# Experts of a routed feed-forward layer rebuilt: one set of 64 places for a pair, weights in 4 KB pieces

## Chip, cores and metric

The kernel runs on one core of one Trainium2 chip. The number that counts is the device time of one execution, in microseconds (us). Work is spread over the core's engines: PE (matrix products; PEld is its loading of the stationary operand), DVE and ACT (elementwise work), POOL, and SP, whose queue issues nearly all transfers from memory (HBM). Sixteen DMA engines move the data. Products land in PSUM banks (128 partitions x 512 float32) and are read from there by DVE or ACT.

## What is computed

One layer over 256 tokens of width 1024. Its first half (norm, input products, stick-breaking attention, retention, gated output products) is not touched by the change. The second half is a mixture of 16 experts in 4 groups: a token picks its best group and in it its best two experts, and the result is normed once more.

```python
    group_probs = jax.nn.softmax(group_logits, axis=-1)
    p_group, g_sel = lax.top_k(group_probs, 1)
...
    top_vals, top_idx = lax.top_k(in_group, TOP_K_IN_GROUP)
    gate = jax.nn.softmax(top_vals, axis=-1) * p_group
    expert_id = g_sel * EXPERTS_PER_GROUP + top_idx
    combine = jnp.sum(jax.nn.one_hot(expert_id, N_EXPERTS, dtype=jnp.float32) * gate[..., None], axis=1)
...
    for e in range(N_EXPERTS):
        hidden = jax.nn.silu(xt @ w_exp_gate[e]) * (xt @ w_exp_up[e])
        y = y + combine[:, e:e + 1] * (hidden @ w_exp_down[e])
...
    return rms_norm(h, norm_final_g)
```

Each expert has two weights of 1024 x 512 (gate, up) and one of 512 x 1024 (down), in float32: 6.3 MB an expert, 100.7 MB for all 16. Every expert's weights are read once, whatever the routing.

## The kernel before

**Memory and loads.** On-chip memory is cut into 25 slots of 8 KB a partition (1 MB), handed out first freed, first used (`take`, `give`). All weights are split into tiles of one slot. `plan` puts a tile on a list in the order of its use, and `pump` issues the next ones on SP's queue (L161) as long as slots are free; a tile's slot is freed (`drop`) by the last product that reads it. While the dense half runs, the table `LIMIT` caps how many tiles are loaded; after the routing the cap is lifted (L861). The experts' tiles follow the dense ones: for each pair of experts 4 tiles of gate, 4 of up, 4 of down, 96 in all. A tile holds 256 rows of both experts of the pair, as two DMAs of 512 KB (`both`, L444). Partition p takes rows p and 128+p of the 256, so each contiguous piece in memory is one row of 512 numbers, 2 KB. The last tile is cut into four DMAs. Eight DMAs are in flight at most.

**Routing.** From the logits DVE makes a 0/1 mask of the chosen experts, PE counts them by a product with a triangular table, and `rank` gives each token its place in each expert (64 places, `CAP`). `onehot` turns ranks into 0/1 matrices `pt` for four experts at a time. `cnt` is the largest count of an expert (L875).

**The experts**, two at a time (`experts`, `up_to_hidden`), in the order of the code, which is the order on every engine:

- `gather` (L893) multiplies the rows by `pt` and puts the rows of four experts x 64 places, transposed, into `xgt`. The first two pairs' rows come from the float32 rows themselves (`gather_pair`, L906), the later ones from rows in two parts `hn` (`rows_in_parts`).
- `proj` (L961) makes the gate product and then the up product. The two experts of the pair stand in the two halves of one bank (64 partitions each): 16 matmuls a product, 32 records in the trace, since each float32 matmul makes two.
- `place_shares` (L942) gives each place its row's norm and its share; ACT applies silu (L1017), DVE multiplies with the up product (L1049), PE transposes the hidden rows (L1054) and ACT copies them out (L1055). `place_table` (L935) transposes the 0/1 matrix for the way back (L939, L940).
- `down` (L980) makes the two halves of 512 columns one after the other, each into its own bank, again with the two experts in the two halves of the partitions. `split_y` splits each bank in two parts `y2` (ACT L546, DVE L547).
- `scatter` (L997) multiplies by the table and adds a pair's rows onto four banks `F` that hold the running sum; a pair's scatter stands between the next pair's up and down products.

After seven pairs the engines read `cnt` into a register and `tc.If(most > CAP)` (L1147) decides over further rounds for an expert of more than 64 tokens. The eighth pair and the final norm stand behind that block, so that every engine passes it:

```python
    experts(True)
...
    most = nc.values_load(cnt[0:1, 0:1], min_val=0, max_val=T)
    assert not loads
    with tc.If(most > CAP):
...
    ht = up_to_hidden(NP - 1, final_gain)
```

At the end each of the four quarters of the sum (two blocks of tokens `tb`, two halves of columns `q`) is squared by ACT (L1177), the norm is a power on POOL (L1196), and ACT and DVE scale the rows that two queues store (L1201 to L1204).

Of the kernel before, what the change touches and what calls it, by code (L numbers as in the profile page):

```python
# [9 lines left out]
F32 = mybir.dt.float32  # L10
# [17 lines left out]
# weight tiles loaded by the start of a unit of the dense products, at most  # L28
# [6 lines left out]
# columns of the packed constant table (one row per partition)  # L35
# [35 lines left out]
# columns of the packed parameters  # L71
# [7 lines left out]
R_N = 228  # L79


def pack(ins):
# [9 lines left out]
        ins["norm_final_g"].reshape(8, P).T,  # L92
    ], axis=1))
# [3 lines left out]
def layer(ctx: ExitStack, tc, cst, dec, prm, x, w_in, w_gate, w_sb_out, w_ret_out,  # L97
# [108 lines left out]
    units = []  # L206

    def dense_a(tag, w, c0, ncol, rhs, evac, nk=KC):
        """out^T [cols, tokens]: weights stationary, tokens moving."""
# [10 lines left out]
    def dense_b(tag, w, c0, widths, lhs, evac, pieces=1, hook=None):  # L220
        """out [tokens, cols]: tokens stationary, weights moving."""
# [222 lines left out]
    def both(w, i, r, cs, cut=False):  # L444
        """256 rows of the weights of a pair of experts."""
        e = [rows(w[0, 2 * i + j], 256 * r, 2, cs.start, 512) for j in range(2)]
        if cut:
            return [((slice(None), j, k), e[j][:, k]) for k in range(2) for j in range(2)]
        return [((slice(None), j), e[j]) for j in range(2)]

    for i in range(NE // 2):
        for which, w in (("g", w_exp_gate), ("u", w_exp_up)):
            for r in range(4):
                plan((which, i, r), [P, 2, 2, 512], both(w, i, r, slice(0, 512)))
        for q in range(2):
            for r in range(2):
                plan(("d", i, q, r), [P, 2, 2, 512], both(w_exp_down, i, r, slice(512 * q, 512 * q + 512),
                                                          (i, q, r) == (NE // 2 - 1, 1, 1)))
    n_expert = 12 * (NE // 2)
    expert_loads = loads[-n_expert:]  # L460

# [499 lines left out]
    def proj(i, which, ps, ahead=None):  # L961
        for r in range(4):
            if ahead:
                ahead(r)
# [263 lines left out]
```

## Time and profile before

| | |
|---|---|
| median of 3 runs | 484.58 us (484.14 to 484.59) |
| span of the profiled execution | 482.5 us |
| around the span (484.58 - 482.5) | 2.1 us |
| busy share of the span: PE, PEld, DVE, ACT, POOL | 96%, 65%, 41%, 35%, 5% |
| mean granted PE clock, as a share of full speed | 0.987 |
| read from HBM | 140.93 MB |
| experts (first gather to the end) | 249.4 to 482.5 us |

The page gives each engine's busy share, then the span in 40 slices with the granted PE clock and the DMA traffic. PE is busy in nearly every slice. That alone doesn't say that PE sets the time: records of matmuls are pipelined, and a stage is read from its waits. In the slices from 300 to 446 us the DMA engines move 386 to 388 GB/s without a break; then they stop before the end, while the chain of work that ended last runs over PE.

### The profile page before, as it was taken

To read this page: it belongs to the slowest core of one execution; us is meant where nothing else is said; L and a number is where in the kernel's file an instruction comes from. 1 tells how busy PE (TensorE), PEld (TensorE's weight loads), DVE (VectorE), ACT (ScalarE), POOL (GpSimd) and SP (SyncE) were. 2 spreads that over 40 slices of the span, in tenths; PEclk is the share of its full clock that TensorE was granted. 3 is DMA by queue.
4 is the path that set the end of the run, shared out by engine and by line. 5 is a ranking of instruction groups with operands and counts; after the bars stand their busy time and mean duration, and the time that the engine had idled before them with its cause. 6 is when DMAs were issued, how large, how long until landed. Compare 5 with 4: busy or idle time off the path is not lost. (4 is left out here: it accounts for less than half of the span.)

```text
span 482.5 us, 6985 instructions
## 1 busy us (share of the span) xinstructions
PE 462.2 (96%) x2799; PEld 314.4 (65%) x2799; DVE 199.4 (41%) x370; ACT 170.5 (35%) x247; POOL 21.9 (5%) x36
## 2 busy tenths in 40 slices
PE   7899999999999999999999999999999999994993
PEld 6699778888899999999974444543353436341231
DVE  3756488454467755786363121412121112111003
ACT  3633787876555654445321113011010101110023
POOL 2300111000012000000010000000000000000000
PEclk9999999999999999999999999999999999998897
DMA  7999975248020599977998999999999999999902
GB/s 276 353 384 395 383 248 175 88 122 314 1 88 1 185 351 387 385 263 254 392 316 298 382 332 378 386 385 387 387 387 387 386 388 386 387 387 385 337 0 88
DMA packets 83143, 142.51 MB, mean 295 GB/s; under 512 B 3872, under 2 KB 24480, under 8 KB 82976
## 3 DMA queue, kind: packets, MB, share of 16 engines
q1 hardware_dynamic: 82672, 141.35, 82.3%
q10 hardware_dynamic: 432, 0.64, 0.4%
q8 instruction: 24, 0.39, 0.3%
q14 instruction: 15, 0.12, 0.1%
HBM read 140.93 MB, written 1.05 MB: 294 GB/s over the span
## 5 line engine op out<-in xcount | busy, mean ns | idle before, releaser
L970 PE MATMUL p<-b,b 128*64 128x512 f32 x512 | 116.4, 603 | 7.3 <-PEq L1147 6.2
L251 DVE TENSOR_TENSOR b<-b,b 128x1024 fp32r<-128x1024 f32 x72 | 88.7, 1240 | 71.8 <-ACT b L249 70.7
L292 PE MATMUL p<-b,b 128*128 128x512 f32 (+1 forms) x504 | 102.4, 358 | 0.7 <-ACT b L249 0.5
L249 ACT ACTIVATE b<-b 128x1024 fp32r<-128x1024 f32 x72 | 75.5, 1056 | 77.3 <-PE p L280 46.0
L292 PEld LDWEIGHTS p<-b,b 128*128 128x128 f32 x504 | 82.3, 189 | 14.8 <-ACT b L249 0.9
L970 PEld LDWEIGHTS p<-b,b 128*64 128x64 f32 x512 | 36.0, 138 | 76.0 <-issue 72.6
L279 PE MATMUL p<-b,b 128*128 128x256 f32 x288 | 71.6, 286 | 0.0
L280 PE MATMUL p<-b,b 128*128 128x256 f32 x288 | 70.7, 283 | 0.0
L985 PE MATMUL p<-b,b 128*64 128x512 f32 x256 | 56.7, 595 | 0.0
L279 PEld LDWEIGHTS p<-b,b 128*128 128x128 f32 x288 | 55.1, 191 | 0.5
L280 PEld LDWEIGHTS p<-b,b 128*128 128x128 f32 x288 | 55.2, 192 | 0.0
L282 PE MATMUL p<-b,b 128*128 128x256 f32 x288 | 41.1, 283 | 0.0
L985 PEld LDWEIGHTS p<-b,b 128*64 128x64 f32 x256 | 17.7, 137 | 32.9 <-issue 30.5
L282 PEld LDWEIGHTS p<-b,b 128*128 128x128 f32 x288 | 37.4, 192 | 0.0
L547 DVE SCALAR_TENSOR_TENSOR b<-p,b 128x512 fp32r<-128x512 f32 (+1 forms) x20 | 12.7, 635 | 57.5 <-ACT b L546 53.6
L1017 ACT ACTIVATE b<-p,share 128x512 f32<-128x512 f32 x8 | 5.5, 688 | 75.2 <-DVE share L949 75.2
L546 ACT ACTIVATE b<-p 128x512 fp32r<-128x512 f32 (+1 forms) x20 | 11.0, 552 | 54.9 <-PE p L985 54.2
L1049 DVE SCALAR_TENSOR_TENSOR b<-p,share,b 128x512 f32<-128x512 f32 x8 | 6.0, 751 | 49.1 <-PE p L970 49.1
L1055 ACT ACTIVATE b<-p 128x512 f32<-128x512 f32 x8 | 4.8, 599 | 52.2 <-PE p L1054 52.2
L949 DVE TENSOR_REDUCE share<-p 128x3 f32<-128x9 f32 x8 | 1.3, 167 | 43.6 <-PE p L946 43.6
L1001 PE MATMUL p<-b,S 128*128 128x512 f32 x64 | 19.1, 420 | 0.3
L1001 PEld LDWEIGHTS p<-b,S 128*128 128x128 f32 x64 | 10.8, 188 | 9.1 <-issue 6.5
(171 smaller groups left out, 357.9 us busy)
## 6 DMA issues: line engine op xcount, KB each, us to landing
b<-in_w_exp_gate SPq DMA_DIRECT2D x64, 512.0 KB, 10.8
b<-in_w_exp_up SPq DMA_DIRECT2D x64, 512.0 KB, 10.8
b<-in_w_exp_down SPq DMA_DIRECT2D x62, 512.0 KB, 10.7
b<-in_w_in SPq DMA_DIRECT2D x17, 1024.0 KB, 14.5
b<-in_w_gate SPq DMA_DIRECT2D x8, 1024.0 KB, 5.3
b<-in_w_ret_out SPq DMA_DIRECT2D x4, 1024.0 KB, 4.9
b<-in_w_out SPq DMA_DIRECT2D x4, 1024.0 KB, 11.0
b<-in_w_sb_out SPq DMA_DIRECT2D x2, 1024.0 KB, 9.3
```

What stands on the lines that cost most here:

```text
L249: act.activation(hi, raw, AF.Copy)
L251: tt(lo, raw, hi.bitcast(F32), op=ALU.subtract)
L279: pe.matmul(ps, wh[:, k, cs], h[:, k, :], start=k == 0, stop=False)
L280: pe.matmul(ps, wh[:, k, cs], l[:, k, :], start=False, stop=False)
L282: pe.matmul(ps, wl[:, k, cs], h[:, k, :], start=False, stop=k == nk - 1)
L292: pe.matmul(ps[tb], kth(a, k)[:, tb * P:(tb + 1) * P], b[:, j, :], start=n == 0 and k == 0, stop=n == 2 and k == KC - 1)
L546: act.activation(hi, src, AF.Copy)
L547: stt(lo, src, 1.0, hi.bitcast(F32), op0=ALU.mult, op1=ALU.subtract)
L970: pe.matmul(ps[64 * j:64 * j + 64, :], xgt[:, c, o:o + 64], w[:, j, k, :], start=c == 0, stop=c == KC - 1)
L985: pe.matmul(y[64 * j:64 * j + 64, :], ht[:, f, 64 * j:64 * j + 64], w[:, j, k, :], start=f == 0, stop=f == 3)
L1001: pe.matmul(F[q][tb], work["S"][:, tb * P:(tb + 1) * P], y2[0][:, h, cs], start=first and h == 0, stop=last and h == 1, skip_group_check=True)
L1049: stt(b, u, out[0][:, 0:1], b, op0=ALU.mult, op1=ALU.mult)
```

## The change

The experts' part is rebuilt; the dense half stays as it is.

- **Places for a pair.** A new mask `either` (the larger of the two masks of a pair, one DVE instruction for each block of tokens) takes the place of the mask in the counting. 64 places are now shared by the two experts of a pair: a token that picks either or both has one place. `rank` has 8 columns, `cnt` is the largest count of a pair. The share of a token in an expert it didn't pick is 0. By the reference's routing of its inputs the eight pairs hold 57, 61, 46, 46, 59, 53, 52 and 51 tokens.
- **Gathers.** Four pairs fit into `xgt`. The first four are gathered from the float32 rows (`gather_two`, the same work as `gather_pair` for two pairs before); the other four by one `gather` ahead of pair 4, where there were three. The stationary operand of a gather is now every second column of the rows.
- **4 KB pieces.** Gate and up tiles give partition p the rows 2p and 2p+1, one piece of 4 KB (hence the new order of the features, `features` and `R_FP`). A down tile is 256 rows of one expert, all 1024 columns, one DMA of 1 MB with pieces of 4 KB. The last tile is cut in two.
- **Down in one bank.** Both experts' down products are summed in one bank; the two halves of 512 columns stand in its two halves of the partitions. One split (ACT, DVE) for a pair instead of two, and the scatter's products contract over 64 rows instead of 128.
- **Pairs overlapped.** Order on PE: half of gate(i), shares and table of pair i and the transposes of pair i-1, the rest of gate(i), down(i-1), half of up(i), scatter(i-1), the rest of up(i). The loads are planned in that order (`STEPS`). Pair 4 has its gather and down(3) ahead of its gate.
- **The end in both blocks.** `cnt` is read before the first gather (L1205). `tc.If(most <= CAP)` comes after the last up product; the two last down products and the final norm stand in that block, and once more in the other one, behind the further rounds.

The core of the diff:

```diff
-    for i in range(NE // 2):
-        for which, w in (("g", w_exp_gate), ("u", w_exp_up)):
-            for r in range(4):
-                plan((which, i, r), [P, 2, 2, 512], both(w, i, r, slice(0, 512)))
...
+    def plan_rows(which, w, i):
+        for r in range(4):
+            e = [w[0, 2 * i + j][256 * r:256 * r + 256].rearrange("(p k) n -> p k n", k=2) for j in range(2)]
+            plan((which, i, r), [P, 2, 2, 512], [((slice(None), j), e[j]) for j in range(2)])
+
+    def plan_down(i):
+        for r in range(4):
+            e = rows(w_exp_down[0, 2 * i + r // 2], 256 * (r % 2), 2, 0, D)
+            cut = (i, r) == (NP - 1, 3)
+            plan(("d", i, r), [P, 2, D],
+                 [((slice(None), k), e[:, k]) for k in range(2)] if cut else [(slice(None), e)])
+
+    STEPS = [("g", 0), ("u", 0)]
+    for i in range(NP - 1):
+        if i == 3:
+            STEPS += [("d", i), ("g", i + 1), ("u", i + 1)]
+        elif i == NP - 2:
+            STEPS += [("g", i + 1), ("u", i + 1), ("d", i)]
+        else:
+            STEPS += [("g", i + 1), ("d", i), ("u", i + 1)]
+    STEPS.append(("d", NP - 1))
...
+        m2 = mk[:, tb].rearrange("p (i j) -> p i j", j=2)
+        tt(either[:, tb], m2[:, :, 0], m2[:, :, 1], op=ALU.max)
...
+    def features(c2, c):
+        return slice(256 * c2 + c, 256 * c2 + 256, 2)
...
+    def down(i, hook=None):
+
+        y, ht = bank("g"), work["ht"][i % 2]
+        for r in range(4):
+            if hook:
+                hook(r)
+            w = raws[("d", i, r)]
+            j = r // 2
+            for k in range(2):
+                f = 2 * (r % 2) + k
+                for q in range(2):
+                    pe.matmul(y[64 * q:64 * q + 64, :], ht[:, f, 64 * j:64 * j + 64], w[:, k, 512 * q:512 * q + 512],
+                              start=r == 0 and k == 0, stop=r == 3 and k == 1)
+            after(("d", i, r))
+        hilo(y2[0][:, 0, :], y2[0][:, 1, :], y)
+
+    def scatter(i, tb, first=False, last=False):
+
         for h in range(2):
...
+            for q in range(2):
+                r = slice(64 * q, 64 * q + 64)
+                pe.matmul(F[q][tb], work["S"][i % 2][r, tb * P:(tb + 1) * P], y2[0][r, h, :],
+                          start=first and h == 0, stop=last and h == 1, skip_group_check=True)
...
+        for i in range(1, NP):
+            def in_gate(r):
+                if r == 2:
+                    tables(i)
+                    if i != 4:
+                        hidden(i - 1)
+
+            def in_up(r):
+                if r == 2 and i < NP - 1:
+                    for tb in range(NB):
+                        scatter(i - 1, tb, first and i == 1)
...
+            if i == 4:
+                pt = onehot(1)
+                gather(1, pt, [0, 1])
+                hidden(3)
+                gather(1, pt, [2, 3])
+                down(3)
+            places(i)
+            g = gate(i, in_gate)
+            silu(i, g)
...
+            if i != 4 and i < NP - 1:
+                down(i - 1)
+            up(i, in_up)
+
+    def tail():
+        i = NP - 1
+
+        def in_first(r):
+            if r == 2:
+                hidden(i)
+
+        def in_second(r):
+            if r == 1:
+                for tb in range(NB):
+                    scatter(i - 1, tb)
+
+        down(i - 1, in_first)
+        down(i, in_second)
...
+    most = nc.values_load(cnt[0:1, 0:1], min_val=0, max_val=T)
+    head(True)
+    assert not loads
+    kept = (dict(raws), dict(held), list(free))
+    with tc.If(most <= CAP) as fits:
+        tail()
+        finish()
+
+    with fits.Else():
```

Three places in the order of the instructions on PE. First the middle of a pair, before: the end of an up product (L970), the scatter of the pair before (L1001) with the transposes between (L1054, L939). The down product of the same pair follows.

```order
L970 MATMUL p_3313<-b_3138,b_2461 64x512 x4
L970 MATMUL p_3313<-b_3145,b_2461 64x512 x4
L1001 MATMUL p_2488<-b_2654,S_2587 128x512 x2
L1001 MATMUL p_2489<-b_2654,S_2587 128x512 x2
L1054 MATMUL p_3347<-identr_80,b_2586 128x128 x4
L1001 MATMUL p_2490<-b_2654,S_2587 128x512 x2
L1001 MATMUL p_2491<-b_2654,S_2587 128x512 x2
```

The same pair's stretch now: the transposes of the hidden rows (L1020) in the middle of a gate product (L1000), the down product of the pair before (L1034), the up product, and in its middle the scatter (L1044).

```order
L1020 MATMUL p_3197<-identr_80,b_2596 128x128 x4
L1000 MATMUL p_3171<-b_2958,b_2460 64x512 x4
L1000 MATMUL p_3171<-b_2965,b_2460 64x512 x4
L1034 MATMUL p_3218<-b_2975,b_2596 64x512 x4
L1034 MATMUL p_3218<-b_2981,b_2596 64x512 x4
L1034 MATMUL p_3218<-b_3003,b_2596 64x512 x4
L1034 MATMUL p_3218<-b_3009,b_2596 64x512 x4
L1000 MATMUL p_3249<-b_3066,b_2460 64x512 x4
L1000 MATMUL p_3249<-b_3073,b_2460 64x512 x4
L1044 MATMUL p_2487<-b_2629,S_2597 128x512
L1044 MATMUL p_2489<-b_2629,S_2597 128x512
```

The transposes moved from the gap between up and down into the next pair's gate product, the down product behind that, and the scatter alternates between the banks of the two halves of columns. Second, PE at the choice of the block, before: the scatter of the seventh pair, the read of `cnt`, the branch, and behind it the rounds that are jumped over.

```order
L985 MATMUL p_3523<-b_3302,b_2586 64x512 x4
L1001 MATMUL p_2488<-b_2654,S_2587 128x512 x2
L1001 MATMUL p_2489<-b_2654,S_2587 128x512 x2
L1001 MATMUL p_2490<-b_2654,S_2587 128x512 x2
L1001 MATMUL p_2491<-b_2654,S_2587 128x512 x2
L1145 TENSOR_LOAD cnt_2471
L1147 COMPARE_AND_BRANCH
```

And now: the last up product, the branch, and right behind it the two last down products of the block that is kept.

```order
L1000 MATMUL p_3423<-b_3283,b_2460 64x512 x4
L1209 COMPARE_AND_BRANCH
L1034 MATMUL p_3456<-b_3294,b_2596 64x512 x4
L1034 MATMUL p_3456<-b_3300,b_2596 64x512 x4
L1020 MATMUL p_3465<-identr_80,b_2596 128x128 x4
L1034 MATMUL p_3456<-b_3323,b_2596 64x512 x4
```

The work that runs stands next to the branch now, and the jump over the other block (an unconditional branch of L1209) comes behind the last scatter. Third, PE at the start of the experts, before, with the semaphores that an instruction waits for: the gather of pair 0 (L912) follows the last filler products (L203).

```order
L203 MATMUL p_2455<-ones_78 128x128
L912 MATMUL p_2492<-pt_2450,b_74 128x128 [waits PE_49]
L912 MATMUL p_2492<-pt_2450,b_74 128x128 [waits DVE_49]
L912 MATMUL p_2492<-pt_2450,b_74 128x128 x2
L912 MATMUL p_2499<-pt_2450,b_74 128x128 x4
```

And now: the read of `cnt` stands ahead of the gather and waits for DVE.

```order
L205 MATMUL p_2454<-ones_78 128x128
L1205 TENSOR_LOAD cnt_2470 [waits DVE_49]
L933 MATMUL p_2505<-pt_2449,b_74 128x128 [waits PE_49]
L933 MATMUL p_2505<-pt_2449,b_74 128x128 [waits DVE_49]
L933 MATMUL p_2505<-pt_2449,b_74 128x128 x2
```

PE's whole queue of the experts now stands behind that read; so does the queue of DVE, ACT, POOL and SP, each with a read of its own.

## Rows read from the trace of the kernel before

**Rows 1.** Stretches: length, busy us (count) by engine, granted clock, DMA share, GB/s.

```profile
170.00:178.00 8.00, 8.00 (x69) 8.00 (x68) 4.06 (x7) 4.07 (x6) 0.00 (x0) 1.00 1.11 349
184.00:206.00 22.00, 22.00 (x186) 22.00 (x184) 15.29 (x25) 8.89 (x12) 0.00 (x0) 1.00 1.05 386
304.00:432.00 128.00, 127.90 (x645) 55.08 (x645) 23.89 (x55) 13.68 (x24) 0.00 (x0) 1.00 1.05 387
...
46.00:47.00 1.00, 1.00 (x7) 0.83 (x6) 0.62 (x1) 0.34 (x1) 0.00 (x0) 1.00 1.12 440
```

**Rows 2.** Timeline of SP's queue: start us, us, line, operation, count.

```profile
240.85 13.42 SPq L161 DMA_DIRECT2D b<-in_w_exp_down  x8
256.34 9.07 SPq L161 DMA_DIRECT2D b<-in_w_exp_gate  x8
```

**Rows 3.** The branch's line: duration ns min/median/max, first and last start us.

```profile
L1147 SPq EVENT_SEMAPHORE  x8: 17/17/17, 457.6 to 459.2; - x8
...
L1147 DVEq COMPARE_BRANCH  x1: 72/72/72, 437.8 to 437.8; - x1
...
L1147 PEldq COMPARE_BRANCH  x1: 6192/6192/6192, 438.5 to 438.5; - x1
```

**Rows 4.** Timeline of PE, pairs 2 to 6, start us, us.

```profile
303.77 4.40 PE L900 MATMUL p<-pt,b 128*128 128x256 f32 x32
...
419.58 0.21 PE L946 MATMUL p<-cmb,b 128*128 128x9 bf16 x2
419.72 7.09 PE L970 MATMUL p<-b,b 128*64 128x512 f32 x32
426.74 1.20 PE L1001 MATMUL p<-b,S 128*128 128x512 f32 x4
427.78 0.61 PE L1054 MATMUL p<-identr,b 128*128 128x128 f32 x4
...
429.16 0.28 PE L939 MATMUL p<-idb,b 128*128 128x128 bf16 x2
429.37 7.09 PE L985 MATMUL p<-b,b 128*64 128x512 f32 x32
436.39 2.53 PE L1001 MATMUL p<-b,S 128*128 128x512 f32 x8
```

**Rows 5.** Timeline of PE from the branch on, with the wait before each.

```profile
445.16 4.50 PE L970 MATMUL p<-b,b 128*64 128x512 f32 x9 [6.24 <-PEq L1147]
450.76 5.37 PE L970 MATMUL p<-b,b 128*64 128x512 f32 x23 [1.10 <-issue]
...
463.21 0.65 PE L1166 MATMUL p<-identr,par 128*128 128x128 f32 x4
...
465.81 7.09 PE L985 MATMUL p<-b,b 128*64 128x512 f32 x32
```

**Rows 6.** Stretch 444 to 456 us, columns as in rows 1.

```profile
444.00:456.00 12.00, 9.74 (x32) 2.67 (x32) 0.49 (x2) 0.00 (x0) 0.00 (x0) 0.75 1.03 379
```

**Rows 7.** Timeline at the start of the experts, and the read of the count on PE.

```profile
249.42 1.86 PEld L912 LDWEIGHTS p<-pt,b 128*128 128x128 f32 x16 [0.23 <-PE p L203]
249.43 2.05 PE L912 MATMUL p<-pt,b 128*128 128x128 f32 x16
...
250.27 0.15 DVE L875 CAST cnt<-cmax 128x1 int32<-128x1 f32 x1
...
L1145 PEldq TENSOR_LOAD <-cnt x1: 492/492/492, 437.9 to 437.9; - x1
```

**Rows 8.** Timeline of PE: an attention score, products over 64 rows.

```profile
48.88 0.92 PE L560 MATMUL z<-b 64*128 64x256 f32 x8
```

**Rows 9.** The chain that ended last, in order of time: start us, us.

```profile
465.88 7.07 PE p L985 x32
...
474.94 0.70 ACT b L1177 x2
...
477.65 0.72 ACT b L1201
```

More of the change, by code (lines that the diff above doesn't have):

```diff
@@ L993, in split_y, with gate @@
-    def split_y(y, q):
-        cs = slice(512 * q, 512 * q + 512)
-        hilo(y2[0][:, 0, cs], y2[0][:, 1, cs], y)
-    def scatter(tb, q, last=False, first=False):
-        cs = slice(512 * q, 512 * q + 512)
-        for h in range(2):
-            pe.matmul(F[q][tb], work["S"][:, tb * P:(tb + 1) * P], y2[0][:, h, cs], start=first and h == 0, stop=last and h == 1,
-                      skip_group_check=True)
-    def rows_onto(q):
+            after((which, i, r))
+    def gate(i, hook=None):
+        g = bank("g")
+        proj(i, "g", g, hook)
+        return g
@@ L1100, in shares @@
+                for q in range(2):
+                    pe.matmul(F[q][tb], identr, hn[h][:, tb, 512 * q:512 * q + 512], start=False, stop=False,
+                              skip_group_check=True)
     def shares():
@@ L1139, in shares, with head, ahead, early @@
         yield
-    experts(True)
-    gfin = take([P, 2048])[:, 0:D]
+    def head(first):
+        pt = pt0 if first else onehot(0)
+        fetch = (lambda c2: gather_two(0, pt, c2)) if first else (lambda c2: gather(0, pt, [c2]))
+        parts = shares() if first else iter(())
+        fetch(0)
+        def ahead(r):
+            if r < 3:
+                fetch(r + 1)
+            next(parts, None)
+        def early(r):
+            if r == 1:
+                places(0)
+            if r == 2:
+                tables(0)
+                silu(0, g0)
+        g0 = gate(0, ahead)
+        up(0, early)
+        if first:
+            gather_two(1, pt, 0)
+            gather_two(1, pt, 1)
+        for i in range(1, NP):
[8 more added lines that the diff above has]
+                        scatter(i - 1, tb, first and i == 1)
+                    if first and i == 3:
+                        rows_onto()
+                if r == 2 and i == NP - 1:
+                    for q in range(2):
+                        final_gain(q)
+            if i == 4:
[7 more added lines that the diff above has]
+            silu(i, g)
+            if first and i == 1:
+                gather_two(1, pt, 2)
+                gather_two(1, pt, 3)
+            if i != 4 and i < NP - 1:
+                down(i - 1)
+            up(i, in_up)
```

308 lines of the change are left out of this document (113 added, 195 removed).

## The prediction

> **What bounds the kernel now.** Times are in us from the start of the profiled execution's span (482.5; the median of the runs, 484.58, is 2.1 above it, and I add those 2.1 at the end).
>
> I read the stretches by time first. From 304 to 432 PE is busy in 127.90 of 128 us, but the DMA engines are full too: 387 GB/s without a break [rows 1]. So two lines run side by side, and the next question is which of them ends last. SP's queue shows it: its last eight waits for landed weights, ahead of the branch, end at 459.2 [rows 3], while the chain that ended last runs over PE's last down product, 465.88 + 7.07 = 472.95, then squares and stores [rows 9]. PE thus sets the time, by 13.7 us over the loads. The reader should see both: an edit that shortens only PE gains at most about that much before the loads are late, and one that shortens only the loads gains nothing.
>
> Third, PE's timeline, for what PE does that is no product of weights. Each weight product is a steady 7.09 of 32 records [rows 4]. Between an up product and the down product of one pair lie a scatter and transposes (426.74 to 429.37, 2.63), between gate and up 0.14 (419.58 to 419.72). Three gathers cost over 4 us each; the one shown took 4.40, the two others 4.15 and 4.13. At the branch PE stands still for 6.24 (its branch instruction alone 6192 ns [rows 3]), and the gate product behind it takes from 445.16 to 450.76 + 5.37 = 456.13, 10.97 in place of some 6.97 [rows 5]. The granted clock of 444 to 456 is 0.75, a mean of stretches at 2.4 and at 1.2 GHz, right behind PE's idle time [rows 6]; the 4.0 are the cost of having stood.
>
> **PE's line, part by part** (change of the end of the last down product, 472.95).
>
> - *Gathers.* Three become one; two at 4.1 or more go: −8.2. The remaining one must wait for its 0/1 matrices from DVE, now asked for right there, behind the last up product of pair 3: I estimate 1.4 exposed (+1.4; between 0 and 2).
> - *The middle of a pair.* Before 2.63 + 0.14 = 2.77. Now shares, hidden rows and table stand in the gate product: 0.61 + 0.28 + 0.21 = 1.10 [rows 4], plus 0.05 for turns between shapes, 1.15. Their inputs are ready a half product earlier, so the waits in the 2.63 go; and the silu and multiplication of pair i-1 lie beside half a gate product (3.5). The scatter has eight products of 64 rows in place of eight of 128. If the two halves of the rows run side by side, that is four steps, as the four records at 426.74, which hold PE until 427.78: 1.04, say 1.05. Together 2.2; −0.57 a pair, six pairs: −3.4.
> - Does the side-by-side hold? The nearest row is the attention score, eight records over 64 rows in two halves, 4 of 256 columns and 4 of 128, in 0.92 [rows 8]. A down record of 512 columns takes 7.09/32 = 0.222 with two at a time, so 0.443 alone, 0.865 ns a column; 1536 columns one after the other would be 1.33. So 0.92 speaks for halves that overlap. Bound: not at all, +0.85 for each of seven scatters, +6.
> - *Scatter of pair 6.* It stood open behind its split, 2.53 at 436.39 [rows 4]; now it lies in down(7): −1.5.
> - *Branch.* Behind it stands now the block that runs, so PE passes on instead of jumping: −6.24, and with no idle PE −4.0 on the gate: −10.2. By the reference's routing the pairs have at most 61 tokens, so that block does run. Bound: a branch that isn't taken costs PE as much, +6.2. The jump over the other block comes behind PE's last scatter, with 472.95 to 482.5 of other work still to run: hidden up to some 7. DVE's branch took 72 ns [rows 3]; I take the other engines' jumps as nothing.
> - *Last pair and first.* Before down(7) PE had 463.21 to 465.81 + 0.14 = 2.74 [rows 5]; now the gains (two groups of 0.65), 1.15 and the hidden rows of pair 7, 0.7, in all 3.1: +0.4. Pair 0 loses an open wait for its hidden rows: −0.6 (estimate).
> - *Start.* The first gather ran at 249.43. Now PE must first read the count, which DVE casts at 250.27 + 0.15; it may come 0.2 later for one DVE step more (`either`, on a longer `rank`) or earlier for ranks of half the columns. With the read, 0.49 [rows 7], the gather starts at some 251.2: +1.75. Behind PE's read stands its whole queue. SP's read stands ahead of the experts' later loads only, and slots come free only with the first gates.
> - *Strided columns.* The early gathers and the one of four pairs load every second column as the stationary operand. No row has that. An ordinary load is 1.86/16 = 0.116 [rows 7], and 96 loads are concerned: between 0 and, at double, +11.1. I take 0, since the products that they hide behind (2.05/16 = 0.128) are longer, and nearest are L1166's loads of one repeated element, which don't lengthen their products (0.65 for four [rows 5]).
>
> Sum: −8.2 + 1.4 − 3.4 − 1.5 − 10.2 + 0.4 − 0.6 + 1.75 = −20.35, end at 452.6.
>
> **The line of the loads.** Time of one piece per engine of 16: at 349 GB/s in pieces of 1 KB, 46.9 ns; at 387 in pieces of 2 KB, 84.7 [rows 1]. So 37.7 for each KB and 9.2 fixed; 4 KB would take 160.1, 409 GB/s. The stretch with 8 KB pieces, 440 for 1 us, says that more than 387 is there. A tile of 1.0486 MB takes 2.71 now and 2.56 then. The engines are full from the end of the first wave of slots: the last of them is issued by 254.3 and the next at 256.34 [rows 2], 72 tiles: −10.6. Added: +1.75 for the later start, since the first slots come free later, and about +1 (estimate) for slots held longer, since down weights wait a half pair. 459.2 becomes 451.4. Behind the last half tile PE has 0.9 of products: the end isn't before 452.3.
>
> *A page against the change.* The Trainium skill, "DMA: Bandwidth & Descriptors", section "Where 436 GB/s comes from", says that for HBM to SBUF the HBM side of about 358 GB/s binds; by it larger pieces would bring nothing, and the loads would set 474.5 (rival B). The 387 over 128 us speaks against that bound. The same page has, in the section "iDMA fabric — 4 AXI ports for 8 engines, asymmetric across TPBs", 408.7 GB/s for a stream of 1 MiB DMAs with rows of 4 KiB; no run here has shown that, and a tile would be an estimated 2.57.
>
> **The end.** 482.5 − 472.95 = 9.5 now. One split serves both halves of columns, so all four squares come behind the last scatter, where two of them (0.70 a pair [rows 9]) and their wait lay beside it: +1.0. Both lines end near 452.5; where they cross, each waits a little for the other: 453. 453 + 9.5 + 1.0 = 463.5, and 2.1: **465.5 us**.
>
> **Rivals.**
>
> - *A, the forecast:* 461 to 470, 0.62.
> - *B, 4 KB pieces are no faster than 2 KB.* The loads end at 459.2 + 1.75 = 461.0, the last product at 461.9, time 461.9 + 10.5 + 2.1 = 474.5. For it: 387 is steady, over two stretches, as if it were a ceiling; against it: the step from 349 and the 440. 0.10.
> - *C, PE's line is longer.* Strided loads (+11.1), scatters that don't overlap (+6), a branch that costs though it isn't taken (+6.2), or waits of the transposes in the middle of a gate. Each gives 470 to 477; the first, at full price, 453 + 11 = 464, time 476.6. For it: half the new pieces have no row. 0.17. One rule fits: the Trainium skill, "TensorEngine Tiling (Array Packing)", section "Key Properties", says that a change of tiling mode drains the engine. By it each interruption of a product would cost more than its own work. The two products of the shares, with the turns to their shape and back, hold PE for 0.14 between gate and up [rows 4], so a turn is of the order of 0.1.
> - *F, better:* the waits fall more, or loads run at 420 and PE's start costs nothing: 459 to 461. 0.07.
> - *D, slower than before.* 4 KB pieces go slower, because one piece holds an engine's turn longer while eight DMAs of 1 MB queue. The loads then set the end from a tile of 2.85 (368 GB/s) on: 72 x (2.85 − 2.71) = 10 above B, 484.6. At 349, the lowest rate among the stretches, 72 x 0.30 = 21: 495.8. For it: nothing but that the only long stretches at full load have 1 and 2 KB; against it: rates rise with the piece. 0.04. That the change doesn't do what it says (a pair over 64 tokens, so that the other block runs too) would also land here; the counts exclude it.
>
> **How the numbers follow.** A is likeliest, so its 465.5 is the time. To leave out two in ten, the range runs from 459.5 (F's larger part) to 476 (B and most of C). About 0.2% (1 us) is what a measurement of this kernel can tell from no change. A, B, C and F are all below 483.6, but a crowd of C's costs at once could reach it: faster 0.95, same 0.01, slower 0.04.
>
> **What the changed profile would show.** DMA between 300 and 440 at about 409 GB/s (at 387: B; under 370: D). SP's last landed weights at about 451. PE's branch without 6 us of idle time behind it and a gate product of pair 7 of 7.0 at clock 1.00. One gather of 4.1 ahead of pair 4 with some 1.4 of waiting; the gather of pair 0 at 2.05 (at 4: C). Scatters of about 1.05 (at 1.9: C). The first gather at 251.2. From the last scatter to the end 8.5. Wrong would be the whole balance if PE waited on weights all through the pairs: then only the DMA line counts.

## The result, and the profile after

| | before | after |
|---|---|---|
| median | 484.58 us (484.14 to 485.78) | 467.88 us (466.61 to 468.62) |
| span of the profiled execution | 482.5 us | 466.1 us |
| ratio, 95% interval | | 0.966 (0.964 to 0.967) |

The kernel is 16.7 us faster, 3.4%. The forecast was 465.5, 2.4 us less.

The stretches by time, to be held against [rows 1] (columns as there): two stretches at full load, then the last microseconds of the loads.

```profile
184.00:206.00 22.00, 22.00 (x186) 22.00 (x185) 15.25 (x25) 9.03 (x11) 0.00 (x0) 1.00 1.03 409
304.00:432.00 128.00, 126.00 (x626) 46.70 (x622) 17.43 (x45) 14.20 (x25) 0.00 (x0) 1.00 1.03 409
...
450.00:451.00 1.00, 1.00 (x6) 0.29 (x4) 0.00 (x0) 0.00 (x0) 0.00 (x0) 1.00 0.14 57
451.00:452.00 1.00, 1.00 (x8) 0.40 (x6) 0.00 (x0) 0.00 (x0) 0.00 (x0) 1.00 0.00 0
```

The loads run at 409 GB/s in place of 387 and end in 450 to 451. PE is still busy in 126 of 128 us, and its idle time there isn't spent on weights. So PE's line sets the time again, and the loads have some 2 us to spare.

PE's timeline (start, length, line; in brackets the idle time ahead and who ended it), to be held against [rows 4] and [rows 5]: the start, the gather of four pairs, a pair without a gather, and the end.

```profile
247.38 2.67 PE L205 MATMUL p<-ones 128*128 128x128 bf16 x24
...
251.97 2.12 PE L933 MATMUL p<-pt,b 128*128 128x128 f32 x16 [1.41 <-DVE cnt L895]
...
343.08 3.65 PE L1000 MATMUL p<-b,b 128*64 128x512 f32 x16
347.93 2.41 PE L922 MATMUL p<-pt,b 128*128 128x256 f32 x16 [1.19 <-DVE pt L841]
350.17 0.65 PE L1020 MATMUL p<-identr,b 128*128 128x128 f32 x4
351.12 2.20 PE L922 MATMUL p<-pt,b 128*128 128x256 f32 x16 [0.30 <-DVE b L925]
353.24 7.09 PE L1034 MATMUL p<-b,b 128*64 128x512 f32 x32
...
380.18 3.65 PE L1000 MATMUL p<-b,b 128*64 128x512 f32 x16
...
403.25 3.65 PE L1000 MATMUL p<-b,b 128*64 128x512 f32 x16
...
434.37 3.65 PE L1000 MATMUL p<-b,b 128*64 128x512 f32 x16
437.86 3.60 PE L1034 MATMUL p<-b,b 128*64 128x512 f32 x16
...
447.28 1.19 PE L1044 MATMUL p<-b,S 64*128 64x512 f32 x8
448.40 5.37 PE L1034 MATMUL p<-b,b 128*64 128x512 f32 x24
```

From one second half of a gate product to the next a pair takes 403.25 - 380.18 = 23.07. Around the branch (behind the product that begins at 434.37) PE doesn't stop. The last down product ends at 448.40 + 5.37 = 453.77, where it ended at 472.95. Two things weren't in the forecast. Ahead of the first gather the 24 filler products take 2.67; and from 453.77 to the end there are 12.3 us where the forecast had 10.5.

### The profile page after: what moved, and what is told of

It is laid out like the page before. It is cut to its first block, busy times and chain, and to the rows that moved or that the text cites. A ratio compares the mean times of both kernels' runs of the same rounds, so it can differ in the third digit from the quotient of the medians.

```text
span 466.1 us, 6780 instructions
## 1 busy us (share of the span) xinstructions
PE 446.3 (96%) x2735; PEld 301.4 (65%) x2735; DVE 187.5 (40%) x353; ACT 165.7 (36%) x239; POOL 21.8 (5%) x36
## 4 chain that ended last, share of the span: by engine, by line
PE 93%; DVE 2%; ACT 1%; DMA 1%; issue 1%; POOL 1%; DVEq 0%
PE p L1000 24%; PE p L294 20%; PE p L1034 12%; PE p L281 8%; PE p L284 7%; PE p L282 7%; PE p L933 2%; PE p L1044 2%; PE z L577 1%; PE p L922 1%; PE p L1020 1%; DMA b<-in_x 1%; PE p L205 1%; PE p L679 1%; PE p L620 1%
## 5 line engine op out<-in xcount | busy, mean ns | idle before, releaser
L1000 PE MATMUL p<-b,b 128*64 128x512 f32 x512 | 115.1, 596 | 0.0
L1000 PEld LDWEIGHTS p<-b,b 128*64 128x64 f32 x512 | 35.0, 137 | 66.3 <-issue 63.0
L1034 PE MATMUL p<-b,b 128*64 128x512 f32 x256 | 56.7, 594 | 0.0
L1034 PEld LDWEIGHTS p<-b,b 128*64 128x64 f32 x256 | 18.0, 137 | 35.1 <-issue 33.1
L564 DVE SCALAR_TENSOR_TENSOR b<-p,b 128x512 fp32r<-128x512 f32 (+1 forms) x12 | 7.2, 599 | 75.2 <-ACT b L563 75.2
L563 ACT ACTIVATE b<-p 128x512 fp32r<-128x512 f32 (+1 forms) x12 | 6.3, 522 | 53.4 <-PE p L1034 52.8
L969 ACT ACTIVATE b<-p 128x256 fp32r<-128x256 bf16 x4 | 1.5, 385 | 37.4 <-PE p L968 37.4
L969 ACT ACTIVATE S<-p 128x256 fp32r<-128x256 bf16 x4 | 1.5, 383 | 36.8 <-PE p L968 36.8
L933 PEld LDWEIGHTS p<-pt,b 128*128 128x128 f32 x64 | 7.9, 196 | 4.9 <-issue 4.9
## 6 DMA issues: line engine op xcount, KB each, us to landing
b<-in_w_exp_gate SPq DMA_DIRECT2D x64, 512.0 KB, 10.2
b<-in_w_exp_up SPq DMA_DIRECT2D x64, 512.0 KB, 10.2
```

Source lines behind the costliest of these rows:

```text
L563: act.activation(hi, src, AF.Copy)
L564: stt(lo, src, 1.0, hi.bitcast(F32), op0=ALU.mult, op1=ALU.subtract)
L933: pe.matmul(ps[:, c, :], xt[:, tb, features(c2, c)], pt[:, tb, 2 * i:2 * i + 2].rearrange("p e s -> p (e s)").bitcast(F32), start=c == 0 a ...
L1000: pe.matmul(ps[64 * j:64 * j + 64, :], xgt[:, c, o:o + 64], w[:, j, k, :], start=c == 0, stop=c == KC - 1)
L1034: pe.matmul(y[64 * q:64 * q + 64, :], ht[:, f, 64 * j:64 * j + 64], w[:, k, 512 * q:512 * q + 512], start=r == 0 and k == 0, stop=r == 3 a ...
```

## The experiments

Twelve kernels ran. Times are medians; "end" is the time from the last record of the last down product to the end of the span. PE's clock in the routing differs from execution to execution (below), by which a time can move by 0.6 to 3.6 us, so small effects are read from the trace.

**Pieces of 2 KB in the changed kernel.** Same tiles, same order; each transfer takes other rows of the same bytes (the cut of the down tiles into halves of the columns isn't shown):

```diff
-            e = [w[0, 2 * i + j][256 * r:256 * r + 256].rearrange("(p k) n -> p k n", k=2) for j in range(2)]
-            plan((which, i, r), [P, 2, 2, 512], [((slice(None), j), e[j]) for j in range(2)])
+            e = w[0, 2 * i:2 * i + 2, 256 * r:256 * r + 256].rearrange("j (p k) n -> p j k n", k=2)
+            plan((which, i, r), [P, 2, 2, 512], [((slice(None), slice(None), k), e[:, :, k]) for k in range(2)])
```

> The changed kernel with the same tiles, order and layout, but each transfer of a gate or up tile takes one row of both experts and each of a down tile one half of the columns: pieces of 2 KB, 512 KB a transfer (the last tile in four). Theory (the larger pieces carry the loads from 387 to 409 GB/s, and the loads lie some 2 us behind PE's line): 72 tiles x 0.15 = 10.6 later, the last weights land at about 461 in place of 450.6, PE waits for weights from some pair on, and the time is about 476 (474 to 478). Rival (the loads have slack, since pairs overlap and slots come free in another order): no change, 468. Second rival (the order of the loads and not the piece made 409): the rate stays near 409 and so does the time.

Measured 476.65 us, ratio 0.985 (0.982 to 0.988). Stretch, PE's last down product, and PE's waits on the weights of the down products (total, times, longest):

```profile
304.00:432.00 128.00, 125.03 (x614) 45.54 (x610) 17.42 (x45) 14.20 (x25) 0.00 (x0) 1.00 1.05 387
```

```profile
455.92 6.07 PE L1036 MATMUL p<-b,b 128*64 128x512 f32 x24
```

```profile
PE p L1036 <- DMA b<-in_w_exp_down: 1.2, 5, 0.4
```

The rate falls to 387, PE's waits on weights appear from 428 on, one short wait for each tile (the idle part only; products that trickle behind a late tile count as busy), and the last product ends at 461.99. Both rivals of this run fall. The pieces are worth 8.8 us to the changed kernel.

**Pieces of 4 KB in the kernel before**, and nothing else. Its products take the rows of the weights for other rows than they are, so its sums are of other numbers; bytes and products are as many as before:

```diff
-        e = [rows(w[0, 2 * i + j], 256 * r, 2, cs.start, 512) for j in range(2)]
+        e = []
+        for j in range(2):
+            v = w[0, 2 * i + j]
+            if v.shape[1] == D:
+                v = v.rearrange("a (b n) -> (a b) n", n=512)
+            r0 = 256 * (2 * (cs.start // 512) + r) if w is w_exp_down else 256 * r
+            e.append(v[r0:r0 + 256].rearrange("(p k) n -> p k n", k=2))
```

> The kernel before with pieces of 4 KB and nothing else: gate and up tiles take rows 2p and 2p+1, down tiles a contiguous block, so that rows of the weights stand in other places than the products take them for (the sums are of other numbers, the work is the same). Theory (PE sets the kernel before, by 13.7 us over the loads): the rate rises to about 409 GB/s, the loads end near 449, and the time stays within 1 us of 484.6. Rival (PE's waits hide in its steady products, the loads share the bound): faster by 2 us or more.

Measured 482.24 us, 0.996 (0.994 to 0.997): 1.9 less than before, at the edge between theory and rival. The trace shows where. Stretch, and the gate product behind the branch, to be held against [rows 5]:

```profile
304.00:432.00 128.00, 127.90 (x644) 54.75 (x644) 23.84 (x55) 13.12 (x23) 0.00 (x0) 1.00 1.02 406
```

```profile
444.45 8.76 PE L976 MATMUL p<-b,b 128*64 128x512 f32 x32 [6.13 <-PEq L1153]
453.14 0.21 PE L952 MATMUL p<-cmb,b 128*128 128x9 bf16 x2
```

The loads speed up and PE's line from the first gather to the scatter ahead of the branch doesn't change, as the theory has it (186.96 in both, by the starts). But the product behind the branch takes 453.14 - 444.45 = 8.69 in place of 10.97, without the standstill of 1.10 in its middle, though PE stood nearly as long ahead of it (6.13). One stretch behind the branch, in the kernel before and then here (busy us by engine, and the granted clock, DMA share and GB/s at the end):

```profile
448.00:449.00 1.00, 1.00 (x3) 0.00 (x0) 0.00 (x0) 0.00 (x0) 0.00 (x0) 0.50 1.06 385
```

```profile
448.00:449.00 1.00, 1.00 (x6) 0.55 (x5) 0.00 (x0) 0.00 (x0) 0.00 (x0) 1.00 0.05 18
```

Before, the loads still run and PE is at 1.2 GHz until inside 449; here they have all but ended and PE is back at 2.4 GHz from inside 447 on. So 2.3 of the 4.0 that the slow gate cost are gone in this execution, the shortest of ten. Whether that hangs on the loads the runs don't show: the clock had also fallen earlier here, inside 440 in place of 443. A fetch of code that comes late beside full queues would fit the standstill. The same edit thus gives 1.9 in one kernel and 8.8 in the other: what the pieces are worth depends on what stands behind them.

**The end in both blocks in the kernel before**, and nothing else (`last` is the eighth pair and the final norm):

```diff
-    with tc.If(most > CAP):
+    with tc.If(most <= CAP) as fits:
+        last()
+    with fits.Else():
...
+        last()
```

> The kernel before with the eighth pair and the final norm in both blocks, the further rounds in the other one, and nothing else. Theory: PE falls through the branch, 6.24 of standing and 4.0 of a slow gate product go, the end grows by some 1.5 since stores and jump stand ahead of the other block's code: -8.7, about 476. Rival 1 (a branch that isn't taken costs PE as much): 482 to 485. Rival 2 (the loads are late next): the last weights land at 459.2 as before, the last product at 462.7 or later, 477 to 479.

Measured 475.86 us, 0.983 (0.980 to 0.985), where 476 was expected. PE around the branch:

```profile
436.33 2.53 PE L1001 MATMUL p<-b,S 128*128 128x512 f32 x8
438.79 7.09 PE L970 MATMUL p<-b,b 128*64 128x512 f32 x32
...
455.56 7.09 PE L985 MATMUL p<-b,b 128*64 128x512 f32 x32
```

No standstill, no slow product; the last down product ends at 462.65, 10.3 before 472.95 (forecast for this term: 10.2). A branch that isn't taken costs PE nothing that can be seen. But the end grows here too, to 474.2 - 462.65 = 11.55 from 9.55, with squares and stores as in the kernel before.

**The changed kernel without the other block.** No branch; it leaves out the further rounds, which these inputs don't need; the count is still read:

```diff
-    with tc.If(most <= CAP) as fits:
-        tail()
-        finish()
-
-    with fits.Else():
...
+    tail()
+    finish()
```

> The changed kernel without the branch and without the other block (the further rounds are left out, which these inputs don't need); the count is still read at the start. Theory (the end is 12.3 us long in place of 10.5 because the jumps of the engines over the other block and the fetching of code fall among the last stores): the second store on SP issues in 0.35 in place of 1.48, the end shrinks to about 10.5 to 11, the time to 466.3. Rival (the end is longer by the stores and the squares themselves): 467.9, the end stays at 12.3. By both PE's line up to the last down product stays within 0.3, leaving the stretch of slow clock in the routing aside.

Measured 465.59 us, 0.962 (0.959 to 0.966); the interval overlaps the changed kernel's, so the end is read from the trace. PE's last down product and DVE's last scaling here; then the stores of the last microseconds, of this kernel and of the changed kernel (queues of code: packets, MB, share of the engines; stores: size, us to landing):

```profile
447.60 5.37 PE L1034 MATMUL p<-b,b 128*64 128x512 f32 x24
...
457.74 1.49 DVE L1202 SCALAR_TENSOR_TENSOR b<-p,rf,b 128x512 f32<-128x512 f32 x2
```

```profile
out<-b SPq DMA_DIRECT2D x2, 256.0 KB, 2.6
```

```profile
q8 instruction: 2, 0.03, 1.5%
q14 instruction: 4, 0.03, 0.9%
...
out<-b SPq DMA_DIRECT2D x2, 256.0 KB, 4.2
```

```profile
L1203 SPq DMA_DIRECT2D out<-b x2: 348/915/1482, 459.3 to 460.1; - x2
```

The end is 463.2 - 452.97 = 10.2 in place of 12.3 (11.9 in the second execution of the changed kernel, below). In the changed kernel six transfers of code (queues q8 and q14) fall into these microseconds, SP's stores land 1.6 us later, and one store takes 1482 ns to issue where the other takes 348. Without the other block no code is fetched there. So 1.7 to 2.1 of the end come with the other block. The 10.2 - 9.55 = 0.7 that are left are two things: DVE's last scaling ends 459.23 - 452.97 = 6.26 behind the product, where it was 4.94 in the kernel before, since all squares stand behind one split; and behind the scaling are 4.0 in place of 4.6.

**The read of the count at pair 4.** The changed kernel ran again beside this run and the next two: 468.21 us, ratio 0.967 (0.964 to 0.969).

> The changed kernel as it is, as the measure for the three kernels beside it. Expected 467.9 (466.5 to 468.7), the last down product at 452.8 to 453.8 after the stretch of slow clock in the routing did or did not occur, and 12.3 us from there to the end.

```diff
-    most = nc.values_load(cnt[0:1, 0:1], min_val=0, max_val=T)
     head(True)
...
                 pt = onehot(1)
+                if first:
+                    read.append(nc.values_load(cnt[0:1, 0:1], min_val=0, max_val=T))
                 gather(1, pt, [0, 1])
```

> The changed kernel with the read of the count moved from ahead of the first gather to pair 4, where PE stands 1.19 us for the 0/1 matrices (on DVE behind the making of them). Theory (the read at the start costs PE a wait of 1.4 to 1.6 for the count, and at pair 4 it hides in the other wait): the first gather starts 1.4 to 1.6 earlier, nothing is given back at pair 4, 1.5 faster than the changed kernel, about 466.4. Rival 1 (the read costs its 0.49 there too): 1.0 faster. Rival 2 (the loads, 2 us behind PE, bind next): under 0.7 faster, with waits of PE on weights in the last pair.

Measured 466.21 us, 0.962 (0.960 to 0.964), 2.0 less than the run beside it.

```profile
250.18 2.68 PE L933 MATMUL p<-pt,b 128*128 128x128 f32 x16
...
346.69 2.41 PE L922 MATMUL p<-pt,b 128*128 128x256 f32 x16 [1.19 <-DVE pt L841]
```

The first gather follows the fillers without a wait, and at pair 4 the wait is 1.19 as in the changed kernel, so the read hides in it. The loads don't bind yet.

**The 0/1 matrices earlier:**

```diff
                 if r == 2 and i < NP - 1:
                     for tb in range(NB):
                         scatter(i - 1, tb, first and i == 1)
+                    if i == 3:
+                        later.append(onehot(1))
...
-                pt = onehot(1)
+                pt = later.pop()
```

> The changed kernel with the 0/1 matrices of the last four pairs made by DVE in the middle of the up product of pair 3 rather than behind it. Theory (the wait of 1.19 ahead of the gather of four pairs is DVE's making of them behind the multiplication): the wait falls to some 0.1, 1.1 faster than the changed kernel. Rival (the gather waits for something else at that place, the multiplication or a bank): no change.

Measured 467.30 us, 0.964 (0.961 to 0.966).

```profile
345.51 3.65 PE L1000 MATMUL p<-b,b 128*64 128x512 f32 x16
349.10 2.19 PE L922 MATMUL p<-pt,b 128*128 128x256 f32 x16
```

The wait of 1.19 is gone. The time is 0.9 less than beside it; the intervals overlap, so the trace shows this and the time alone wouldn't. The profiled execution is the longest of the five (468.98). In it the clock in the routing stays at 1.2 GHz from inside 247 to inside 257, so that the first gather itself is slow (2.12 in the changed kernel):

```profile
251.58 3.76 PE L933 MATMUL p<-pt,b 128*128 128x128 f32 x16 [1.41 <-DVE cnt L895]
```

**The stores behind both blocks**, all four on SP, which has no other work then:

```diff
-            act.dma_start(out[0, tb * P:(tb + 1) * P, halves[0]], o[:, tb, halves[0]])
...
-            sp.dma_start(out[0, tb * P:(tb + 1) * P, halves[1]], o[:, tb, halves[1]])
...
+    for tb in range(NB):
+        for q in range(2):
+            sp.dma_start(out[0, tb * P:(tb + 1) * P, halves[q]], o[:, tb, halves[q]])
```

> The changed kernel with the four stores taken out of the two blocks: they stand once behind them, all on SP's queue, so that SP has jumped over the other block long before. Theory (SP's jump, 3.4 us from its branch at 461.9 to its next instruction, and a second store that takes 1.48 us to issue make 2.1 of the 12.3 us of the end): the end shrinks to about 10.5, the time by 1.5 to 2. Rival (the jumps of the other engines hold the end in the same way, or the four stores in one queue cost as much): within 0.5 of the changed kernel.

Measured 466.99 us, 0.964 (0.962 to 0.966). PE's last down product and SP's stores (ns, min/median/max):

```profile
448.36 5.37 PE L1034 MATMUL p<-b,b 128*64 128x512 f32 x24
```

```profile
L1230 SPq DMA_DIRECT2D out<-b x4: 343/374/1504, 458.8 to 461.6; - x4
```

The end is 465.8 - 453.73 = 12.1, no shorter than the 11.9 (466.4 - 454.52) of the run beside it. The median is 1.2 below that run's, between theory and rival and with intervals that overlap; in the traces the whole difference lies ahead of the last product (453.73 against 454.52). SP's own jump is out of the way, but now one of its stores takes 1504 ns. So the theory that SP's jump is the price falls. What holds the end is tied to the other block (the run without it), and is neither SP's jump alone nor the queue of the stores. Which engine's fetch of code it is, no run isolates.

**More filler in the routing**, 20 products of ones where PE waits for DVE:

```diff
     next(best)
+    keep_warm(3)
     logits(lp, 3, [1])
+    keep_warm(2)
```

> The changed kernel with 20 more filler products (of ones, not used) ahead of and behind the last logits' products, where PE waits 0.47 and 0.25 us for DVE; they fit those waits. Theory (the stretch at 1.2 GHz in the routing, from about 247.5 on in most executions, follows PE's thin stretch just ahead of it, busy 0.91 and 0.54 of 245 to 247): granted clock 1.00 from 245 to 252 in the profile, the first gather 1 us earlier, median about 467.1 with less spread. Rival (the thin stretch isn't what lowers it, or the fillers are too few): the stretch is there as before, 468.

Measured 466.80 us, 0.964 (0.962 to 0.966). The routing by stretches of 1 us (PE's busy time first, the granted clock third from the end), in the changed kernel and then here:

```profile
246.00:247.00 1.00, 0.54 (x4) 0.54 (x5) 0.93 (x7) 0.38 (x1) 0.50 (x1) 1.00 1.06 418
247.00:248.00 1.00, 0.75 (x10) 0.67 (x9) 0.89 (x5) 0.00 (x0) 0.06 (x1) 0.74 1.06 336
248.00:249.00 1.00, 1.00 (x13) 1.00 (x11) 0.78 (x4) 0.00 (x0) 0.00 (x0) 0.50 0.85 344
249.00:250.00 1.00, 1.00 (x14) 1.00 (x13) 0.00 (x0) 0.00 (x0) 0.00 (x0) 0.50 1.00 410
```

```profile
246.00:247.00 1.00, 1.00 (x19) 1.00 (x16) 0.90 (x8) 0.26 (x1) 0.56 (x1) 1.00 0.98 385
247.00:248.00 1.00, 1.00 (x23) 1.00 (x21) 0.90 (x5) 0.00 (x0) 0.00 (x0) 1.00 1.07 361
248.00:249.00 1.00, 1.00 (x20) 0.88 (x18) 0.65 (x4) 0.00 (x0) 0.00 (x0) 1.00 1.01 393
```

With PE filled the clock stays at 2.4 GHz (1.00) in the profiled execution, as it does in the two runs below that have the same filler, and from the 24 fillers' start to the first gather it is 250.85 - 247.27 = 3.58 in place of 4.59.

**The last down product by halves of the columns**, each with its own bank and split, as in the kernel before:

```diff
-        down(i, in_second)
+        down_last(in_second)
...
+        for q in range(2):
+            y = bank("g")
...
+                    for j in range(2):
+                        pe.matmul(y[64 * j:64 * j + 64, :], ht[:, f, 64 * j:64 * j + 64], w[:, j, k, :],
+                                  start=f == 0, stop=f == 3)
...
+            hilo(y2[1][:, q, 0, :], y2[1][:, q, 1, :], y)
```

> The changed kernel with the last pair's down product as in the kernel before: one half of the columns after the other, each in its own bank with the two experts in the two halves of the partitions (tiles of the last pair in 2 KB pieces), its own split, and scatters of 128 rows. Theory (all four squares behind one split add about 0.7 to 1.0 to the end): from the last down product to DVE's last scaling 6.2 falls to about 5.0, 1.0 faster, 467.1. Rival (the four tiles in smaller pieces and one more split take it back): no change.

Measured 467.48 us, 0.964 (0.962 to 0.967).

```profile
449.87 5.37 PE L1057 MATMUL p<-b,b 128*64 128x512 f32 x24
...
458.76 1.42 DVE L1241 SCALAR_TENSOR_TENSOR b<-p,rf,b 128x512 f32<-128x512 f32 x2
```

```profile
L1242 SPq DMA_DIRECT2D out<-b x2: 343/346/348, 459.5 to 460.2; - x2
```

DVE's last scaling ends 460.18 - 455.24 = 4.94 behind the product; in the changed kernel it is 460.03 - 453.77 = 6.26 (the row is below). The 1.3 are there in the trace; the time isn't clear of the changed kernel's. SP's two stores issue in some 346 ns each here, yet behind the scaling are 466.3 - 460.18 = 6.1, as in the changed kernel, and the stores land 4.0 to 4.2 us after their issue. So the slow issue of a store isn't what the end hangs on; the late landing is there in every kernel with a block to jump over at its end.

**All four edits together, and with the stores behind the blocks.** The diffs are those above, but the read stands where it hides in the wait of 0.30:

```diff
                 hidden(3)
+                if first:
+                    read.append(nc.values_load(cnt[0:1, 0:1], min_val=0, max_val=T))
                 gather(1, pt, [2, 3])
```

> The changed kernel with four edits together: read of the count at pair 4 (here between the transposes and the second half of the gather), 0/1 matrices earlier, more filler, last down product by halves. Sum of the parts on PE: -1.5 - 1.1 - 1.0 - 1.0 = 463.5. Rival (the loads bind next: their last byte lands at 449 to 450.6 and the last quarter product needs it): PE waits for weights in the last pairs and the time stays at 464.5 to 466.

> The same with the four stores behind both blocks on SP's queue. If SP's own jump is part of the end: 0.5 to 1 below the run beside it. If the fetching of code by the other engines' jumps slows the issue of whatever store stands in its way: the same as the run beside it within 0.4, with one store of SP that takes about 1.5 us to issue.

Measured 464.05 us, 0.957 (0.955 to 0.959), and 464.47 us, 0.958 (0.956 to 0.960). The first is faster than both kernels, by 3.8 to 4.2 than the changed one, where the parts add up to 4.6. Its last pair:

```profile
441.42 2.82 PE L1059 MATMUL p<-b,b 128*64 128x512 f32 x8
444.17 1.20 PE L1074 MATMUL p<-b,S 64*128 64x512 f32 x8
445.29 6.06 PE L1059 MATMUL p<-b,b 128*64 128x512 f32 x24
```

Eight records take 444.17 - 441.42 = 2.75 and 24 take 6.06, where 24 take 5.37 in the run with the halves alone: PE now waits for the last weights. A part of this is the edit's own: the last pair's four tiles come in 2 KB pieces, by the prediction's 0.15 a tile an estimated 0.6 later. Here the two lines meet, and rival and theory of this run are each half right. The stores behind the blocks bring nothing, which fits the run with them alone.

## Why the prediction held, and where it didn't

**The two lines.** The forecast had PE's line end at 452.6, the loads at 451.4, the last product at 453. Measured: 453.77, with the last weights in 450 to 451. The branch, the pieces and the other block were changed alone in a run; the other terms are read off the two timelines, and no run isolates them.

| term | forecast | measured | from |
|---|---|---|---|
| start | +1.75 | +2.5 | 251.97 against 249.43 [rows 7] |
| three gathers to one, with the open wait | -6.8 | -6.6 | before 4.33 + 4.08 + 4.06 by the starts of what follows; after 346.73 to 353.24, less 0.65 of transposes |
| middle of a pair, each | -0.57 | -0.6 | 23.07 against 23.67, half of 385.00 to 436.39 less a gather of 4.06 |
| scatter of pair 6 | -1.5 | -1.4 | 1.12 against 2.53 [rows 4] |
| branch and slow gate | -10.2 | -10.3 | the end in both blocks alone |
| last pair and first | -0.2 | +0.2 | what the terms above leave of 453.77 against 472.95 |
| rate of the loads | 409 GB/s | 409 GB/s | stretches |
| end | +1.0 | +2.8 | 12.33 against 9.55 |

*The pieces.* The rate from two slopes of [rows 1] was met exactly, and rival B's 461.9 for the last product is what the run with 2 KB pieces shows, 461.99. The rule that HBM's side of some 358 GB/s binds (the Trainium skill, "DMA: Bandwidth & Descriptors", section "Where 436 GB/s comes from") doesn't hold for this core: 409 over 128 us. The same page's 408.7 for rows of 4 KiB agrees. That PE set the kernel before, so that faster loads alone could bring little, is shown by the run with 4 KB there.

*The branch.* That its 6.24 and the slow gate's 4.0 both go is shown by the end in both blocks alone. The reading that all of the 4.0 is the price of having stood is too simple: with 4 KB pieces in the kernel before PE stood 6.13, and the product behind cost 1.7 more than its usual 7.0.

*Strided columns and scatters over 64 rows*, rival C: sixteen records of the first gather take 2.12 where they took 2.05, the halves of the large gather 2.41 and 2.20 where a half took about 2.1; a scatter holds PE from 447.28 to 448.40, 1.12. So strided loads cost tenths of a microsecond, and the halves run side by side. The changed kernel didn't run with contiguous columns, so the tenths are read, not isolated.

**The step that was mis-sized is the end.** The prediction said "DVE's branch took 72 ns; I take the other engines' jumps as nothing" and let PE's jump hide behind 7 us of other work. PE's jump did hide: in the changed kernel's line of the branch the branch that PE passes takes 95 ns and the jump behind its last scatter 3630 ns, from 455.2 on, over long before the stores land.

```profile
L1209 PEldq COMPARE_BRANCH  x2: 95/1862/3630, 434.4 to 455.2; - x2
```

The chain that ended last, after:

```profile
455.74 1.84 ACT b L1192 x6
...
458.62 1.41 DVE b L1202 x2
```

DVE's last scaling in the kernel before:

```profile
476.47 1.42 DVE L1203 SCALAR_TENSOR_TENSOR b<-p,rf,b 128x512 f32<-128x512 f32 x2
```

Up to 460.03 it is 6.26 from the last down product; the kernel before needed 476.47 + 1.42 - 472.95 = 4.94. That is the part that was foreseen, +1.3 in place of +1.0. Behind it, until the end, are 6.1 in place of 4.6, and 4.0 without the other block: without it the end is 10.2, where the forecast had 10.5. A branch's own 72 ns say nothing of what it costs. With the block code is fetched in the last microseconds and the stores land later; that the fetches are what delays the stores is read from their falling together, and no run separates the two. The Trainium skill, "Runtime: NRT & Kernel Launch", section "Instruction fetch mechanics", says that a taken branch whose target lies outside the two pages at hand forces a fetch before execution goes on; the six transfers of code in the last microseconds, none without the other block, agree with it.

**The second miss is the clock in the routing.** In the profiled execution it lies at 1.2 GHz from inside 247 to inside 250; the 24 fillers take 2.67 in place of 1.50, and the first gather comes about 1 us later than the read of the count alone makes it (in the run with 2 KB pieces, where the clock held, fillers' start to gather is 3.63, in the kernel before 2.06: +1.6, forecast +1.75). The forecast counted one more step of DVE there, but no change of the clock. PE now waits 0.25 for that step (`either`) ahead of the fillers, where it went on at once. The thin stretch ahead of that wait was there before too, without a fall:

```profile
246.00:247.00 1.00, 0.53 (x5) 0.35 (x4) 0.97 (x7) 0.77 (x2) 0.31 (x1) 1.00 0.96 352
```

Of the eight profiled executions with the changed routing and no more filler seven show the fall, the run with 2 KB pieces doesn't; of the three with the routing before none does. From the fillers' start to the second quarter of the first gate product, the six of the seven that read the count at the start lose 0.6 to 3.6 us against the one that held. Whether the wait of 0.25 brings the clock down no run isolates, since the added filler closes this wait and the one of 0.47 ahead of it together.

In the profiled execution the end is 1.8 over the forecast's 10.5 and the last product 0.8 over its 453; together they are the 2.6 between 466.1 and 463.5, and the median is some 0.2 lower. (463.5 and 2.1 are 465.6, not 465.5.) The 0.8 is the start's. The other terms on PE's line came out 0.4 worse than their sum, and the forecast had added 0.4 for waits where the two lines cross; PE never waited for weights, so that this evened out is luck.

## What to carry to other kernels

Where two resources run close together, forecast both lines to their end, and let an edit count only up to where the other line stands: the same larger pieces were worth 1.9 us in one kernel and 8.8 in the other. Keep the work that runs right behind the branch. Don't count a jump by its own nanoseconds alone: look for transfers of code behind it, above all where stores are about to leave. A register that every engine reads belongs where the engines wait anyhow, not ahead of the critical queue.

## What the runs showed of the hardware

- Larger contiguous pieces go on paying: 349 GB/s at 1 KB, 387 at 2 KB, 409 at 4 KB, the last as a straight line through the other two said.
- A branch that PE took ahead of its work cost 6.1 to 6.2 us, a jump behind its work 3.3 to 3.8 us that hid, and a branch that it passed 95 ns. A jump behind the work isn't free either: with a block to jump over at its end a kernel's end is 1.5 to 2.1 us longer than without.
- In those kernels 256 KB stores land 3.2 to 4.4 us after their issue, without the block 2.4 to 2.9. The issue of one store took up to 1482 and 1504 ns in place of some 350 in some of these executions, and in others not.
- PE's clock fell to 1.2 GHz in the changed routing, where PE is thinly busy (0.54 and 0.75 of two stretches of 1 us), in seven of eight executions; with 0.53 and 0.95 in the kernel before it didn't. 20 products of no use, placed in waits, kept it at 2.4 GHz in three executions, and the kernel with them alone is 1.1 to 1.4 us below the changed kernel's two medians, with intervals that overlap.
